# A normalisation kernel at the pace of its DMA engines: early loads cut into halves of 64 partitions, shared by both queues, with 72 transfers in place of 65

## The chip, the cores and the metric

The kernel runs on one core of a Trainium2 chip. The metric is the device time of one execution in microseconds (us). Each run also has a profile of one execution, whose span is some 1.7 to 2.2 us shorter than the device time, since it leaves out what lies around the program.

## The reference

For each of 4 x 8 x 16 = 512 channels of 256 x 256 float32 values, the mean and variance over the channel are taken, and the channel is normalised and scaled:

```python
def reference(x, gamma):                       # x (4, 8, 16, 256, 256), gamma (8, 16)
    mu = x.mean(axis=(3, 4), keepdims=True)
    var = ((x - mu) ** 2).mean(axis=(3, 4), keepdims=True)
    x_norm = (x - mu) / np.sqrt(var + 1e-5)
    return (x_norm * gamma[None, :, :, None, None]).astype(np.float32)
```

134.2 MB are read and 134.2 MB written; each value is needed once.

## The kernel before

A channel is laid over S = 8 partitions, so 16 channels fill a tile of 128 partitions by 8192 float32 values, 4 MiB. There are 32 such units u. Six tiles ("slots", AHEAD = 6) hold units in flight. A unit is loaded into its slot; VectorE sums it, ScalarE sums its squares, TensorE adds the eight partitions of a channel; VectorE scales the tile in place; ScalarE's queue stores it; when the store has landed, SyncE's queue loads unit u + 6 into the slot.

```python
    slots = [data.tile([P, F], F32, name=f"xt{i}") for i in range(AHEAD)]

    def load(u, queue):
        queue.dma_start(out=slots[u % AHEAD][:], in_=xv[u])

    g_row = singles.tile([1, G * C], F32, name="g_row")
    for u in range(AHEAD):
        if u == 1:
            nc.scalar.dma_start(out=g_row[:], in_=gv[None, :])
        load(u, nc.scalar if u in (1, 3) else nc.sync)
    # ... constants and gamma's columns are cut here
    for u in range(U):
        t = slots[u % AHEAD]
        nc.vector.reduce_sum(out=st[:, u, 0:1], in_=t[:], axis=AX.X)
        # ... squares, the small matmul, the root are cut here
        nc.vector.tensor_scalar(
            out=t[:], in0=t[:], scalar1=ps[:, 0:1], scalar2=scale[:, u : u + 1],
            op0=ALU.add, op1=ALU.mult,
        )
        nc.scalar.dma_start(out=ov[u], in_=t[:])
        if u + AHEAD < U:
            load(u + AHEAD, nc.sync)
```

The transfers of the two hardware queues take eight semaphores in turn (the trace has eight that DMAs raise, 128 or 130 times each, 16 times by a large transfer). A transfer that takes a semaphore again waits until its earlier user has landed. The end of the program waits for the eight one after the other (six wait instructions of SyncE between 582.9 and 624.2 us name all eight).

## Time and profile before

| what | value |
|---|---|
| device time | 626.75 us, median of 3 (626.74 to 627.11) |
| span of the profile | 625.2 us |
| large packets (32 KB, one row of one partition) | 8192, so 512 for each of 16 DMA engines |
| median packet | 1213 ns |
| first packet starts | 1.81 us |

The page's DMA row gives the busy share of the 16 engines in tenths for each of 40 equal slices, and the row under it the GB/s that they moved. The first says that the engines have packets in hand, the second how fast those go.

### The profile page before, as it was taken

The page shows a single profiled execution, that of the slowest core. Times are in us where ns is not written, and L with a number is a line of the kernel's source. Part 1 is how long each engine was busy: PE and PEld are TensorE (multiplying, and loading weights), DVE is VectorE, ACT ScalarE, POOL GpSimd, SP SyncE. Part 2 cuts the span into 40 slices and gives each one's busy share as a digit, 9 for nine tenths or more (in the row PEclk, how much of TensorE's full clock was granted, in tenths as well). Part 3 has the DMA queues.
Part 4 walks back from the last instruction along what each step waited for, and adds up shares of the span by engine and source line. Part 5 has one row for each costly group of instructions (what it writes and reads, how often), then busy time and mean ns, then how long its engine had stood idle before and what let it go on. Part 6 is the DMA issues. An engine that isn't in the chain of part 4 may idle for free.

```text
span 625.2 us, 626 instructions
## 1 busy us (share of the span) xinstructions
PE 21.4 (3%) x80; PEld 19.5 (3%) x80; DVE 443.2 (71%) x162; ACT 238.8 (38%) x98; POOL 1.3 (0%) x9
## 2 busy tenths in 40 slices
PE   2000000000000000000000000000000000000000
PEld 2000000000000000000000000000000000000000
DVE  0699999998867668676687766776667867668620
ACT  0444444444444224443244432344423443224400
POOL 0000000000000000000000000000000000000000
DMA  8999999999999999999999999999999999999998
GB/s 369 436 417 424 434 436 436 436 436 437 434 436 434 426 426 430 434 436 436 436 434 434 436 434 434 430 426 430 434 436 436 436 432 434 436 436 434 426 426 365
DMA packets 9220, 268.46 MB, mean 429 GB/s; under 512 B 1025, under 2 KB 1026, under 8 KB 1026
## 3 DMA queue, kind: packets, MB, share of 16 engines
q10 hardware_dynamic: 4898, 142.61, 52.8%
q1 hardware_dynamic: 4320, 125.83, 46.8%
q14 instruction: 2, 0.02, 0.0%
HBM read 134.22 MB, written 134.22 MB: 429 GB/s over the span
## 4 chain that ended last, share of the span: by engine, by line
another core or an unknown queue 64%; DMA 16%; DVE 13%; SPq 1%; PE 1%; issue 0%; ACT 0%
DMA xt<-in_x_dram 9%; DVE st L103 8%; DMA out_dram<-xt 7%; DVE xt L126 4%; SPq L48 1%; PE ps L112 1%; ACT std L117 0%; DVE nvar L113 0%; DVE rstd L121 0%; DVE scale L123 0%
## 5 line engine op out<-in xcount | busy, mean ns | idle before, releaser
L103 DVE TENSOR_REDUCE st<-xt 128x1 f32<-128x8192 f32 x32 | 277.9, 8684 | 111.2 <-DMA xt<-in_x_dram 111.2
L104 ACT ACTIVATE junk<-xt 128x8192 uint8<-128x8192 f32 x32 | 225.0, 7030 | 272.2 <-DMA xt<-in_x_dram 229.0
L126 DVE TENSOR_SCALAR xt<-xt,ps,scale 128x8192 f32<-128x8192 f32 x32 | 145.6, 4550 | 1.2
L117 ACT ACTIVATE std<-nvar,eps_t 128x1 f32<-128x1 f32 x32 | 9.4, 294 | 79.6 <-DVE nvar L113 79.6
L112 PE MATMUL ps<-st,navg 128*128 128x2 f32 x64 | 17.9, 349 | 568.0 <-DVE st L103 568.0
L112 PEld LDWEIGHTS ps<-st,navg 128*128 128x128 f32 x64 | 16.0, 312 | 569.8 <-issue 569.8
L113 DVE TENSOR_SCALAR nvar<-ps 128x1 f32<-128x1 f32 x32 | 9.2, 287 | 23.8 <-PE ps L112 23.8
L121 DVE RECIPROCAL rstd<-std 128x1 f32<-128x1 f32 x32 | 5.3, 164 | 11.6 <-ACT std L117 11.6
L104 ACT ACTIVATION_READ_ACCUMULATOR junk<-xt 128x1 f32 x32 | 6.0, 186 | 0.0
L123 DVE TENSOR_TENSOR scale<-rstd,g_col 128x1 f32<-128x1 f32 x32 | 5.1, 159 | 1.1
L84 PE MATMUL g_ps<-one,g_rep 1*128 1x1 f32 x16 | 3.5, 346 | 2.9 <-DVE g_rep L79 2.9
L84 PEld LDWEIGHTS g_ps<-one,g_rep 1*128 1x128 f32 x16 | 3.5, 325 | 2.9 <-POOL navg L68 2.9
L90 DVE COPY g_col<-g_ps 128x8 f32<-128x8 f32 x1 | 0.2, 166 | 3.7 <-PE g_ps L84 3.7
L74 ACT ACT_TABLE_LOAD x1 | 1.3, 1283 | 2.2 <-issue 2.2
L79 DVE COPY g_rep<-g_row 1x1024 f32<-1x1024 f32 x1 | 0.7, 681 | 2.1 <-DMA g_row<-in_gamma_dram 2.1
L64 POOL TENSOR_SCALAR_AFFINE_SELECT navg<-navg 128x128 f32<-128x128 f32 x1 | 0.4, 403 | 0.1
L68 POOL TENSOR_SCALAR_AFFINE_SELECT navg<-navg 128x128 f32<-128x128 f32 x1 | 0.4, 398 | 0.1
L63 POOL MEMSET navg<- 128x128 f32 x1 | 0.2, 220 | 0.0
L74 ACT ACTIVATE root_eps<-eps_t 128x1 f32<-128x1 f32 x1 | 0.2, 203 | 0.0
L147 POOL MEMSET const-bfloat16-1.0<- 128x1 bf16 x1 | 0.1, 101 | 0.0
L147 POOL MEMSET const-uint8-127<- 128x1 uint8 x1 | 0.1, 101 | 0.0
L147 POOL MEMSET const-float32-0.0<- 128x1 f32 x1 | 0.1, 98 | 0.3 <-issue 0.3
(3 smaller groups left out, 0.3 us busy)
## 6 DMA issues: line engine op xcount, KB each, us to landing
out_dram<-xt ACTq DMA_DIRECT2D x32, 4096.0 KB, 67.1
xt<-in_x_dram SPq DMA_DIRECT2D x30, 4096.0 KB, 33.8
xt<-in_x_dram ACTq DMA_DIRECT2D x2, 4096.0 KB, 33.3
g_row<-in_gamma_dram ACTq DMA_DIRECT2D x1, 0.5 KB
```

The source lines that it names most:

```text
L48: queue.dma_start(out=slots[u % AHEAD][:], in_=xv[u])
L74: nc.scalar.activation(out=root_eps[:], in_=eps_t[:], func=ACTF.Sqrt)
L79: nc.vector.tensor_copy(out=g_rep[:], in_=g_row[:].rearrange("o (n k) -> o n k", n=NG).unsqueeze(3).to_broadcast([1, NG, K, S]),)
L84: nc.tensor.matmul(out=g_ps[:, n : n + 1], lhsT=g_rep[:, n].rearrange("o k s -> o (k s)"), rhs=one[:], start=True, stop=True,)
L103: nc.vector.reduce_sum(out=st[:, u, 0:1], in_=t[:], axis=AX.X)
L104: square = nc.scalar.activation(out=junk[:], in_=t[:], func=ACTF.Square, accum_out=st[:, u, 1:2],)
L112: nc.tensor.matmul(out=ps[:], lhsT=navg_w, rhs=st[:, u], start=True, stop=True)
L113: nc.vector.tensor_scalar(out=nvar[:, u : u + 1], in0=ps[:, 0:1], scalar1=ps[:, 0:1], scalar2=ps[:, 1:2], op0=ALU.mult, op1=ALU.add,)
L117: nc.scalar.activation(out=std[:, u : u + 1], in_=nvar[:, u : u + 1], func=ACTF.Sqrt, bias=eps_t[:], scale=-1.0,)
L121: nc.vector.reciprocal(out=rstd[:, u : u + 1], in_=std[:, u : u + 1])
L123: nc.vector.tensor_mul(out=scale[:, u : u + 1], in0=rstd[:, u : u + 1], in1=g_col[:, g : g + 1],)
L126: nc.vector.tensor_scalar(out=t[:], in0=t[:], scalar1=ps[:, 0:1], scalar2=scale[:, u : u + 1], op0=ALU.add, op1=ALU.mult,)
```

## The change

Its intent, as I read it, is to bring unit 0 in sooner, by loading it (and unit 2) through both queues at once, and to end on the last of the eight semaphores: with the early loads and unit 6 in halves there are 1 + 12 + 2 + 25 + 32 = 72 = 9 x 8 transfers. The halves are halves of the rows, partitions 0 to 63 and 64 to 127.

```diff
-    def load(u, queue):
-        queue.dma_start(out=slots[u % AHEAD][:], in_=xv[u])
+    def load(u, queue, lo=0, hi=P):
+        queue.dma_start(out=slots[u % AHEAD][lo:hi], in_=xv[u, lo:hi])
...
-    for u in range(AHEAD):
-        if u == 1:
-            nc.scalar.dma_start(out=g_row[:], in_=gv[None, :])
-        load(u, nc.scalar if u in (1, 3) else nc.sync)
+    load(0, nc.sync, 0, P // 2)
+    nc.scalar.dma_start(out=g_row[:], in_=gv[None, :])
+    load(0, nc.scalar, P // 2, P)
+    load(2, nc.sync, 0, P // 2)
+    for h in range(2):
+        load(1, nc.scalar, h * P // 2, (h + 1) * P // 2)
+    load(2, nc.scalar, P // 2, P)
+    for u in range(3, AHEAD):
+        for h in range(2):
+            load(u, nc.sync, h * P // 2, (h + 1) * P // 2)
...
         if u + AHEAD < U:
-            load(u + AHEAD, nc.sync)
+            for h in range(2) if u == 0 else [None]:
+                lo, hi = (0, P) if h is None else (h * P // 2, (h + 1) * P // 2)
+                load(u + AHEAD, nc.sync, lo, hi)
```

## The prediction

> **What bounds the kernel now.** I read the page first (busy shares, the 40 slices, the queues), then the windows view at both ends, then the waits of the DMA queue's engine, and last the single packet and semaphore records of the trace. The page:
>
> ```profile
> PE 21.4 (3%) x80; PEld 19.5 (3%) x80; DVE 443.2 (71%) x162; ACT 238.8 (38%) x98; POOL 1.3 (0%) x9
> ...
> DMA  8999999999999999999999999999999999999998
> GB/s 369 436 417 424 434 436 436 436 436 437 434 436 434 426 426 430 434 436 436 436 434 434 436 434 434 430 426 430 434 436 436 436 432 434 436 436 434 426 426 365
> ...
> q10 hardware_dynamic: 4898, 142.61, 52.8%
> q1 hardware_dynamic: 4320, 125.83, 46.8%
> ```
>
> No compute engine is full: VectorE, the busiest, is idle for 29%. The DMA row has a 9 in every slice but the first and last, and the two queues' packets together (q1 is issued by SyncE, q10 by ScalarE) take 99.6% of the 16 engines' time. The packet records say what that time consists of. There are 8192 large packets, each one 32 KB row of one partition; their median duration is 1213 ns, on both queues, to within a few per cent at the 90th percentile. That is 32768 B / 1.213 us = 27.0 GB/s for an engine, 432 GB/s for sixteen. 8192 / 16 = 512 packets for each engine, and 512 x 1.213 = 621.1 us, of a span of 625.2. So the kernel is a bare stream of rows, and only the ends are anything else:
>
> ```profile
> 0.00:2.00 2.00, 0.00 (x0) 0.00 (x0) 0.00 (x0) 0.00 (x0) 1.27 (x9) 1.00 0.65 164
> ...
> 621.00:622.00 1.00, 0.00 (x0) 0.00 (x0) 0.00 (x0) 0.00 (x0) 0.00 (x0) 1.00 1.21 524
> 622.00:623.00 1.00, 0.00 (x0) 0.00 (x0) 0.00 (x0) 0.00 (x0) 0.00 (x0) 1.00 0.23 98
> 623.00:624.00 1.00, 0.00 (x0) 0.00 (x0) 0.00 (x0) 0.00 (x0) 0.00 (x0) 1.00 0.00 0
> ```
>
> The last two columns are DMA share and GB/s. The first row's packet starts at 1.81 us; the last ends in the 622nd microsecond, after which the end of the program takes 3.0 us. At the end SyncE waits for the last store:
>
> ```profile
> SPq L48 <- DMA out_dram<-xt: 536.6, 26, 61.7
> SPq L158 <- DMA out_dram<-xt: 41.1, 1, 41.1
> ```
>
> The 26 waits of L48 are loads that wait for a buffer's store. They cost nothing, because both rings hold several rows for each engine: a load takes 33.8 us from issue to landing and a store 67.1, against 19.3 us for a unit of load and store (two times eight rows at 1.213 us). The 41.1 us are stores draining alone after the last load (landed 582.8), still at full rate, 128 to 137 packets in each 10 us. The semaphore records show the tail exactly: the wait that holds the last store's semaphore ends at 624.06, three more wait instructions follow at 624.10, 624.16 and 624.22, the drain comes at 624.29.
>
> [...] after two rows of unit 0, rows of queue 10 start at 6.13 and of queue 1 at 7.34, one 1.213 us row apart, so unit 0 lands only at 20.3 us though eight rows alone would need 9.7.[...]
>
> **The change part by part.**
>
> Bytes: unchanged, 512 rows for each engine. A half has 64 rows, four for each engine if all sixteen are still used; 621.1 us of rows remain.
>
> Start: SyncE's first issue still starts at 0.8 us (0.33 to 0.53 us each), and ScalarE still issues gamma first. Nothing comes sooner. Unit 0 needs eight rows of an engine in place of about fifteen, so without any new limit it lands near 1.8 + 0.9 (the first rows took about 2.0 us) + 8 x 1.213 = 12.4 us, not 20.3. Its store can be issued some 15 us later (sum, root and scaling took 20.32 to 35.34), but that store only joins a ring that has loads to work on. Gain on the path: 0, since no engine was waiting for it.
>
> Semaphores: there are eight, and in the trace each transfer waits for the earlier user of its own semaphore (ScalarE's waits of 17 ns; SyncE's waits name two). Thirteen transfers now go out before the first store, in place of seven, so the ninth to thirteenth must wait for the first to fifth to land. At that time SyncE's ring still holds the first halves of units 2 and 3, eight rows for each engine. Cost 0. Store 0 has to wait for the second half of unit 1, about 32 us, against 27.5 when it is ready; the ring of ScalarE then still holds half of unit 2. Cost 0. In the steady state stores wait for the store four before, 67.1 us old against 4 x 19.3 = 77.4: as now.
>
> Tail: 72 = 9 x 8 transfers instead of 65 = 8 x 8 + 1, so the last store's wait is the last one; the three that follow now (624.06 to 624.29, less one step of 0.04) fall away: -0.19 us.
>
> Issue: seven more issues at 0.33 us, on sequencers that have nothing else due: 0.
>
> [...] In the order of the rings, the pairs that run together, four rows each, are 0 low with 0 high, 2 low with 1 low, 3 low with 1 high, 3 high with 2 high; then units 4 and 5 and later 6, half by half, beside stores.[...] In the first and third pair (16 rows) the halves are opposite, but packets alternate on each engine, and the sixteen engines run nearly in step (their second rows start within 0.5 us of one another), so they are likely to be all on the low half and then all on the high half[...]. There is no slack to absorb it, the engines being full to the end.
>
> **The rivals.**
>
> A, [...]the row stays at 1.213 us, and the result is 626.75 - 0.19 = 626.6. For it: the change looks like the work of somebody who saw halves do no harm, since the semaphore part is worth only 0.2 us[...]
>
> B, [...]the engines fall out of step elsewhere: 626.6 + 19.4 = 646.0.[...]
>
> C, [...]the engines stay in step: up to 626.6 + 67.9 = 694.5; with the spread taken off (about 0.2 us for each of the 40 rows, my estimate from the start times) about 686. For it: the records show that the engines keep step.
>
> D, the new semaphore waits run a ring dry: one ring empty costs nothing while the other has rows; both would have to be, and I count at least four rows left in each. I give this under 1 us.
>
> E, earlier unit 0 really shortens the run: no view shows a wait of the DMA engines for it; at most a part of the slow rows at 40 to 50 us (queue 1's mean 1338 ns over 80 rows, 0.6 us for each engine). This gives 626 at best.
>
> **Range and chances.** I give A (with D and E) 0.41, B and C together 0.58. The two groups don't touch, so a single number is a choice: I take B, 646, which lies between the others[...]. The range runs from A's 626.2 to a little short of C, 684. Over 2% slower begins at 639.3, which B and C pass and A doesn't: slower 0.58, within 2% 0.41, faster (under 614.2, below the 621.1 us of rows) 0.01.
>
> **What would show it.** [...]in the changed profile the DMA row stays 9 while GB/s falls in the first five or six slices[...], and row packets take over 2 us there; unit 0 lands nearer 20 than 12.4 us. [...]GB/s 430 and more from the second slice, unit 0 at about 12.4 us, and first store landing at about 61 instead of 64.4. Semaphores: SyncE waits on landed loads from 2 to about 32 us, with no dip in the DMA row. Tail: about 0.04 us from the last store's wait to the drain. After about slice 8 all should be as before, a unit each 19.3 us. I am wrong in the main if rows keep 1213 ns in halves, and wrong in another way if slices go under 9.

What the forecast says of half rows rested on a claim that no trace of the kernel before shows, so the claim and the terms that came from it are cut. The terms were guesses: 19.4 us for the second and fourth pair, up to 19.4 us for the first and third, and up to 29.1 us beside stores, in sum 19.4 to 67.9 us. Rival B's 646.0, the number given, is 626.6 with 19.4 us of them, and rival C's 694.5 is 626.6 with all 67.9. In "What would show it", the first sentence has the signs of slow half rows (A is wrong), the second those of half rows at 1.213 us (A is right).

## The result, and the profile after

The changed kernel takes 686.82 us (median of 4, 683.88 to 688.60), the kernel before 626.87 us (median of 4). The ratio is 1.0951, with a 95% interval of 1.0913 to 1.0990: 9.5% slower. Ratios here are the mean time of one kernel's fast runs over that of the other's of the same rounds, so not quite the ratio of the medians that are quoted. The results are correct.

The page of the kernel after, busy shares, DMA row and GB/s, queues:

```profile
PE 21.4 (3%) x80; PEld 19.5 (3%) x80; DVE 443.7 (65%) x162; ACT 238.8 (35%) x98; POOL 1.3 (0%) x9
...
DMA  9999999999999999999999999999999999999997
GB/s 213 209 191 214 214 318 335 341 358 404 437 438 437 431 427 433 431 437 437 437 431 429 431 433 437 437 435 433 431 431 431 435 438 435 431 433 431 431 437 320
...
q10 hardware_dynamic: 4930, 142.61, 51.7%
q1 hardware_dynamic: 4400, 125.83, 47.7%
```

The compute engines did the same work. The DMA row has a 9 in every slice but the last: no queue ran dry. But GB/s is half of before in the first five slices (0 to 86 us) and three quarters in the next four or five; from slice 11 on it is as before. So the engines are as busy as before and slower.

The windows view at the same places, first before, then after (columns: stretch, its length, busy time of PE, PEld, DVE, ACT, POOL with counts, clock, DMA share, GB/s):

```profile
12.00:30.00 18.00, 0.56 (x2) 0.50 (x2) 8.93 (x2) 7.12 (x2) 0.00 (x0) 1.00 1.01 437
...
50.00:78.00 28.00, 1.12 (x4) 1.01 (x4) 25.64 (x11) 14.83 (x6) 0.00 (x0) 1.00 1.00 431
...
110.00:130.00 20.00, 0.56 (x2) 0.50 (x2) 18.82 (x7) 12.06 (x4) 0.00 (x0) 1.00 0.98 421
200.00:220.00 20.00, 0.56 (x2) 0.50 (x2) 14.50 (x6) 8.07 (x4) 0.00 (x0) 1.00 1.01 436
```

```profile
12.00:30.00 18.00, 0.00 (x0) 0.00 (x0) 1.83 (x1) 1.84 (x1) 0.00 (x0) 1.00 1.05 226
...
50.00:78.00 28.00, 0.56 (x2) 0.50 (x2) 8.90 (x2) 7.12 (x2) 0.00 (x0) 1.00 1.00 207
...
110.00:130.00 20.00, 0.56 (x2) 0.50 (x2) 15.50 (x6) 7.33 (x4) 0.00 (x0) 1.00 1.00 328
200.00:220.00 20.00, 0.56 (x2) 0.50 (x2) 14.50 (x6) 8.08 (x4) 0.00 (x0) 1.00 1.02 441
```

The second to last column is about 1.00 in all eight lines (it can pass 1, since this view counts a packet whole where it starts), and only the last differs. The packet records say the same for single rows. In the kernel after, rows between 9.3 and 16.5 us, where SyncE's queue has a low half and ScalarE's a high half, take 2.36 us (48 rows, 2.35 to 2.42); from 20 to 68 us the median is 2.55 us; after 160 us it is 1.213 again.

Adding it up: the rows' time over 16 engines is 622.5 us before and 679.9 us after, a difference of 57.4 us. Of that, 39.4 us were added before 80 us, by 32 rows of each engine, and 17.9 us between 80 and 160 us, where 24 half rows run beside stores (these two parts are the packets' time above 1.213 us a row, after less before). The spans differ by 59.4 us. The other 2 us are a first packet that starts at 2.14 us, not 1.81, and engines that finish less evenly at the end. So all but some 2 us of the loss lies in row packets that are longer.

The waits of SyncE's queue, after:

```profile
SPq L48 <- DMA out_dram<-xt: 537.2, 26, 54.7
...
SPq L48 <- DMA xt<-in_x_dram: 53.0, 4, 19.9
```

The second line is new: the four waits for a semaphore's earlier user. They fall where the DMA row has its 9, so they look free here; the first experiment, which keeps them, shows it. At the end the last store's wait ends at 683.68 and the drain follows at 683.72, 0.04 us later instead of 0.23 us.

### The profile page after: what moved, and what is told of

It is laid out like the page before. It is cut to its first block, busy times and chain, and to the rows that moved or that the text cites. A ratio compares the mean times of both kernels' runs of the same rounds, so it can differ in the third digit from the quotient of the medians.

```text
span 684.6 us, 646 instructions
## 1 busy us (share of the span) xinstructions
PE 21.4 (3%) x80; PEld 19.5 (3%) x80; DVE 443.7 (65%) x162; ACT 238.8 (35%) x98; POOL 1.3 (0%) x9
## 4 chain that ended last, share of the span: by engine, by line
another core or an unknown queue 75%; DMA 10%; DVE 8%; SPq 1%; issue 1%; PE 0%; ACT 0%; ACTq 0%; DVEq 0%
DMA xt<-in_x_dram 10%; DVE st L109 6%; SPq L48 1%; DVE xt L132 1%; PE ps L118 0%; ACT std L123 0%; DVE nvar L119 0%; DVE rstd L127 0%; DVE scale L129 0%; ACTq L53 0%; DVEq L109 0%
## 5 line engine op out<-in xcount | busy, mean ns | idle before, releaser
L118 PE MATMUL ps<-st,navg 128*128 128x2 f32 x64 | 17.9, 349 | 629.9 <-DVE st L109 611.5
L118 PEld LDWEIGHTS ps<-st,navg 128*128 128x128 f32 x64 | 16.0, 311 | 631.7 <-issue 597.9
## 6 DMA issues: line engine op xcount, KB each, us to landing
xt<-in_x_dram SPq DMA_DIRECT2D x25, 4096.0 KB, 38.8
```

Source lines behind the costliest of these rows:

```text
L118: nc.tensor.matmul(out=ps[:], lhsT=navg_w, rhs=st[:, u], start=True, stop=True)
```

## The experiments

**Theory P**: how long a row takes depends on the partitions that its transfer writes, and transfers to 0 to 63, or to 64 to 127, are slow (rows of 2.36 to 2.55 us in the kernel after). The reason for it is shown by no run; row times of 4.85 us are guesses. P has two forms, which part where the two queues carry opposite halves: by the moment (slow if all engines are on the same half at once, in step) or by the mean (opposite halves even each other out). **Rivals**: T, more transfers and their semaphore waits; H, the addresses read in HBM; N, transfers of few partitions are slow as such. Fourteen kernels ran. Row times below are medians of the packet records.

### The same 72 transfers, cut along the columns (`cols`)

```diff
     def load(u, queue, lo=0, hi=P):
-        queue.dma_start(out=slots[u % AHEAD][lo:hi], in_=xv[u, lo:hi])
+        lo, hi = lo * (F // P), hi * (F // P)
+        queue.dma_start(out=slots[u % AHEAD][:, lo:hi], in_=xv[u, :, lo:hi])
```

> The changed kernel with every half cut along the columns (128 partitions, 4096 columns each) in place of the rows: same 72 transfers, same order, same queues, same semaphores. Theory P[...]: the cost of the change is gone, 626.4 to 626.9 us, packets of 16 KB at about 607 ns, unit 0 landed near 12.4 us, and the tail is about 0.2 us shorter. Rival T (more transfers and the semaphore waits between them cost the time): it stays near 686 us.

Measured: 627.88 us against 627.07, ratio 1.0013 (0.9997 to 1.0030). The page's GB/s:

```profile
GB/s 367 427 396 451 418 436 424 432 436 435 431 435 436 435 433 435 435 435 433 433 435 429 429 427 431 435 435 433 435 435 433 433 435 435 435 433 435 435 427 352
```

The slices that were near 210 are near 430, packets of 16 KB take 611 ns, and SyncE's share of unit 0 lands at 10.6, ScalarE's at 15.5 us. With number, order, queues and semaphores the same, T is out: the cost is in the cut along the partitions. Earlier data of unit 0 brought nothing.

### Only units 0 and 2 in row halves (`shared_only`)

```diff
+    load(0, nc.sync, 0, P // 2)
+    nc.scalar.dma_start(out=g_row[:], in_=gv[None, :])
+    load(0, nc.scalar, P // 2, P)
+    load(2, nc.sync, 0, P // 2)
+    load(1, nc.scalar)
+    load(2, nc.scalar, P // 2, P)
+    for u in range(3, AHEAD):
+        load(u, nc.sync)                     # and unit 6 whole
```

> Only units 0 and 2 in row halves on both queues, all other loads whole (67 transfers). Theory P with engines in step (each half row takes about twice 1.213 us whatever the other queue does): 16 half rows for each engine, 16 x 1.2 = 19 us, 646 us. Theory P with engines out of step[...]: unit 0's halves are opposite and cost 0, unit 2's halves beside a whole unit cost about 4.85 us each, 636 us. Rival T, by its share of two of the seven extra transfers: about 644 us, so this run parts only the two forms of P.

Measured: 647.23 us, ratio 1.0321 (1.0301 to 1.0342). Sixteen half rows cost 20 us: unit 0's opposite halves cost about as much as the others. The form by the mean (636) misses.

### Opposite halves only (`opposed`), and shifts (`opposed_shift`, `opposed_one`)

```diff
+    nc.scalar.dma_start(out=g_row[:], in_=gv[None, :])
+    for u in range(4):
+        load(u, nc.sync, 0, P // 2)
+        load(u, nc.scalar, P // 2, P)
+    for u in range(4, AHEAD):
+        load(u, nc.sync)                     # and unit 6 whole
```

> Units 0 to 3 in row halves, always the low half on SyncE's queue and the high half on ScalarE's, units 4 and 5 whole: the two queues never write the same half[...]. Theory P out of step: 627 us. Theory P in step (the engines take turns between the rings at the same moments, so all are on the low half, then all on the high half): 32 half rows for each engine at 2.36 instead of 1.21 us, +37 us, 663 us. Rival T: four of seven extra transfers, 661 us.

Measured: 665.91 us, ratio 1.0619 (1.0598 to 1.0640), rows of 2.40 us: +39 us for 32 half rows. Two of its windows:

```profile
12.00:30.00 18.00, 0.00 (x0) 0.00 (x0) 1.84 (x1) 1.85 (x1) 0.00 (x0) 1.00 1.05 226
30.00:50.00 20.00, 0.56 (x2) 0.50 (x2) 14.43 (x6) 8.06 (x4) 0.00 (x0) 1.00 0.98 210
```

A high half on the other queue gives a low half next to nothing (2.40 us against the 2.55 of equal halves). The two shifted kernels add one line ahead of unit 0:

```diff
+    nc.sync.dma_start(out=slots[5][64:96:4], in_=xv[5, 64:96:4])   # opposed_shift
+    nc.sync.dma_start(out=slots[5][64:65], in_=xv[5, 64:65])       # opposed_one
```

> As the run with opposite halves, but before unit 0 one extra load of eight rows[...] on SyncE's queue, which gives one row to eight engines only and so puts them one row behind the others. If the lockstep is the cause[...]: row packets fall from 2.36 towards 1.21 us and the run ends at 627 to 640 us. If [...]the shift doesn't last, 660 to 665 us. Rival T has one transfer more: about 670 us.

> As the run with opposite halves, with one extra row (one engine alone, partition 64, rewritten later) ahead on SyncE's queue. The shift of eight engines changed nothing[...]. If being out of step doesn't help, all sixteen keep 2.37 us and only one engine is late. Total either way 660 to 670 us, since the slowest engine ends it.

Measured: 667.98 us, ratio 1.0652 (1.0631 to 1.0673), and 682.05 us (one run). The semaphore records show that the shift of eight engines worked in part: eight increments of ScalarE's first half come at 21.3 to 21.7 us and eight at 22.4 to 23.1. So eight engines lag by about half a row. Still rows take 2.38 us in the median of both kernels, and between 12 and 78 us none takes less than 2.36 (up to 2.56 where a queue has two rows in a row). No engine got faster by being late. (Most of the 14 us that `opposed_one` lies above the other come late: SyncE's rows after 160 us average 1.264 us there; why, I can't say.)

### A middle piece of 64 partitions (`middle`)

```diff
+    for u in range(AHEAD):
+        for lo, hi in ((0, 32), (32, 96), (96, 128)) if u < 2 else ((0, P),):
+            load(u, nc.sync, lo, hi)
```

> Units 0 and 1 in three row pieces on SyncE's queue alone: rows 0 to 31, 32 to 95, 96 to 127; the rest whole. The middle piece has 64 partitions like a half[...]. Theory P[...]: rows of the middle piece 1.213 us, rows of the outer pieces about 2.4 us: eight slow rows for each engine, 8 x 1.2 = 9.7 us, 636.5 us. Rival N (any transfer of fewer than 128 rows is slow, by its count of rows or its descriptors): all rows 2.4 us, +19 us, 646 us.

Measured: 640.29 us, ratio 1.0211 (1.0192 to 1.0230), "unclear", since the interval holds the 2% line. Rows of the middle pieces take 1.218 us, those of the outer pieces 2.56 us where they don't overlap a piece of another kind. N is out: 64 partitions that lie across both halves are as fast as a whole tile (1.213 us). The packets above 1.213 us add 9.5 us over the kernel before, as expected; the other 3.5 us or so are a gap at the end, told below.

### The same HBM rows to other partitions (`swap`, wrong result)

```diff
+    def piece(u, p, r, n):
+        nc.sync.dma_start(out=slots[u][p:p + n], in_=xv[u, r:r + n])
+
+    piece(0, 32, 0, 64)
+    piece(0, 0, 64, 32)
+    piece(0, 96, 96, 32)
+    piece(1, 0, 32, 64)
+    piece(1, 64, 0, 32)
+    piece(1, 96, 96, 32)
+    for u in range(2, AHEAD):
+        load(u, nc.sync)
```

> Wrong result on purpose: in unit 0 the rows of HBM that made the low half (0 to 63) go to partitions 32 to 95, in unit 1 rows 32 to 95 go to partitions 0 to 63; the rest of both in pieces of 32. SyncE's queue alone. Theory P (the side of SBUF decides): the first four rows of each engine in unit 0 take 1.213 us, those of unit 1 2.4 to 2.56 us; 4 + 8 slow rows, +14.6 us, 641 us. Rival H (the side of HBM decides, by the addresses that the sixteen engines read at once): the first four rows of unit 0 are slow and those of unit 1 fast.

Measured: 656.03 us (one run). In unit 0 the first rows (HBM rows of the low half, partitions 32 to 95) take 1.217 us in the median, those that start between 4 and 7 us; in unit 1 (rows 32 to 95 of HBM to partitions 0 to 63) they take 2.35 to 2.57 us, those that start between 16.9 and 25.3 us. H is out: the partitions written decide. The total is 15 us above the expectation for two other reasons: some rows after 80 us are slow (5.3 us for an engine, unexplained), and the gap at the end is larger:

```profile
630.00:640.00 10.00, 0.56 (x2) 0.50 (x2) 8.82 (x5) 4.27 (x3) 0.00 (x0) 1.00 0.39 167
```

Here the DMA share itself falls. With all early loads on one queue, later loads queue up on SyncE's ring (whole loads land 69.8 and 73.4 us after their issue in the median of `middle` and `swap`, against 33.8), and stores come through fast. Counted by rows, 3.4 stores are still queued when the last load's rows end in the kernel before, 1.5 in `middle` and 1.0 in `swap`; the last unit's compute, 15.05 us, is as long as 1.55 stores of eight rows. What the stores don't cover stands open. In the kernel before, the last store is issued at 597.9 us, 16 us before the store ahead of it lands; in `middle` at 625.8, 1.8 us after it landed. One queue alone need not bring the gap: `every_other` and `sixteen`, below, load on SyncE's queue alone too, have 2.0 and 1.9 stores left, and lose under 1 us at the end. What sets the split of the backlog was not tested.

### Few partitions at a time (`eight`, `sixteen`)

```diff
+    for j in range(4):                                          # eight
+        nc.sync.dma_start(out=slots[0][j:32:4], in_=xv[0, j:32:4])
+    for lo, hi in ((32, 40), (40, 48), (48, 64), (64, 128)):
+        load(0, nc.sync, lo, hi)

+    for lo in (0, 64, 16, 80, 32, 96, 48, 112):                 # sixteen
+        load(0, nc.sync, lo, lo + 16)
```

> Unit 0 on SyncE's queue in small pieces: four transfers of eight rows[...] (eight engines, one row each), two of eight neighbouring rows[...], one of sixteen neighbouring rows[...], then the high half. Theory P: [...]1.2, then 4.85, 4.85, and 2.4 us. Rival N (few partitions are slow as such): the first four kinds are as slow as a half, or slower, 2.4 us and more.

> Unit 0 as eight transfers of sixteen neighbouring rows, one row for each engine, on SyncE's queue, in the order 0, 64, 16, 80, 32, 96, 48, 112.[...] If what counts is the moment: rows of 4.85 us, +29 us, 656 to 660 us. If an engine evens out its rows over neighbouring transfers: rows near 1.2 us, 627 to 632 us. If two transfers run into one another: between, 2.4 us, about 637 us.

Measured: 652.33 and 652.68 us (one run each). In `eight` the first rows, of every fourth partition from 0 to 31, take 1.37 us in the median with the start in it (1.21 at least), so low partitions alone are not slow. The later transfers overlap, so their rows test no single transfer: by the landing times, the other eight engines begin rows of partitions 48 to 63 at 6.5 us. Of the two transfers of eight neighbouring rows, rows of the first then take about 5.0 us and of the second 3.8. The high half, expected at 2.4 us, takes 3.8 to 4.7 beside them (2.43 after them), though those write low partitions alone; and rows of the whole unit 1 take 3.3 to 3.6 us between 26 and 36 us, while half of the engines are still on the high half. The page's GB/s, in slices of 16.3 us:

```profile
GB/s 143 143 355 435 435 435 427 443 423 439 428 433 435 431 440 425 445 421 431 437 431 439 427 441 427 441 423 431 437 431 439 425 445 423 437 431 429 439 411 290
```

So it seems that slow rows slow those beside them, to other partitions too; no run tests this apart. In `sixteen` every row takes 4.50 us (4.485 to 4.507 from the second transfer on), where 4.85 was a guess; the windows view has

```profile
12.00:22.00 10.00, 0.00 (x0) 0.00 (x0) 0.00 (x0) 0.00 (x0) 0.00 (x0) 1.00 0.91 105
```

a quarter of the rate at a DMA share of 0.91. Neighbouring transfers don't even each other out: the next one always writes the other half, and the rows still take 4.50 us.

### Every other partition (`every_other`)

```diff
+    for u in range(2):
+        for h in range(2):
+            nc.sync.dma_start(out=slots[u][h::2], in_=xv[u, h::2])
+    for u in range(2, AHEAD):
+        load(u, nc.sync)
```

> Units 0 and 1 in two transfers each, of every other row to every other partition[...], on SyncE's queue alone.[...] Theory P in step[...]: rows of about 2.4 us, 16 x 1.2 = 19 us, and up to 4 us more at the end as in the run with the middle piece, where the single loading queue left the last store late: 646 to 650 us. Theory P by the mean[...]: rows 1.213 us, 627 to 631 us.

Measured: 628.22 us, ratio 1.0021 (0.9992 to 1.0051), rows of 1.213 us:

```profile
12.00:22.00 10.00, 0.00 (x0) 0.00 (x0) 8.52 (x1) 7.12 (x2) 0.00 (x0) 1.00 0.97 419
```

The 2.4 us expected in step rested on a guess at which rows of a transfer an engine takes. The records don't name a packet's engine, so that stays open; what is shown is that these 64 partitions cost nothing.

### Halves in turn on one queue (`in_turn`), and with a lag (`in_turn_lag`)

```diff
+    for j in range(4):                                          # in_turn_lag alone
+        nc.sync.dma_start(out=slots[5][64 + j:96:4], in_=xv[5, 64 + j:96:4])
+    for u in range(2):                                          # both
+        for h in range(2):
+            load(u, nc.sync, h * P // 2, (h + 1) * P // 2)
+    for u in range(2, AHEAD):
+        load(u, nc.sync)
```

> Control: units 0 and 1 in row halves, low, high, low, high, all on SyncE's queue, other loads whole; only gamma on ScalarE's. In step: all sixteen engines write the low half, then all the high half: 16 half rows at about 2.5 us, +20 us and up to 4 us more for a late last store, 646 to 652 us. If an engine evens out its rows over the four of a transfer and more, it would be 627 to 631 us.

> The control with four extra loads of eight rows ahead on the same queue (eight engines, one row each per load[...], rewritten later): these eight engines start the first low half four rows later, when the others go on to the high half. If the phase decides[...], all half rows take 1.213 us; the eight engines still have four rows more, 4.9 us: 632 to 637 us. If phase doesn't decide[...], 2.4 to 2.5 us stay: 651 to 658 us.

Measured: 662.73 and 664.09 us (one run each). Rows take 2.56 us in both, and 2.36 to 2.43 (2.39 to 2.53 with the lag) where a half follows the other half. The totals lie 10.7 and 6.1 us above what was expected. In the control, rows before 80 us add 19.7 us over the kernel before, as expected; slow rows after 80 us add another 6.9 us (unexplained), and the rest, about 9 us, is mostly a wider gap at the end. The two faults make the totals a poor measure here, so the row times decide. The lag was smaller than planned: the small transfers' issues of 0.7 us each and the first rows' start ate it up, and the two groups of engines land 1 to 2 us apart, not four rows. So this is a weak test, but that lag, too, made no row faster.

### Halves beside stores alone (`beside_stores`)

```diff
-            load(u + AHEAD, nc.sync)
+            for lo, hi in ((0, 64), (64, P)) if u < 3 else ((0, P),):
+                nc.sync.dma_start(out=slots[u % AHEAD][lo:hi], in_=xv[u + AHEAD, lo:hi])
```

> The kernel before, whole early loads, with units 6 to 8 alone in row halves: 24 half rows for each engine, all beside stores. In the changed kernel such rows cost 18.0 us for 24 (0.75 us each, load and store packets together). If that is the term's size: 645 us. If it is the full lockstep of the prediction, 29 us: 656 us. If halves beside stores are free: 627 us.

Measured: 650.10 us, ratio 1.0371 (1.0321 to 1.0420). 24 half rows cost 23 us, 0.97 us each, more than the 0.75 of the changed kernel and less than a full 1.2. Between 80 and 160 us SyncE's rows average 1.98 us and the stores beside them 1.36, so a small part of a half row's time is won back beside stores, and a part of the cost shows on the stores' packets.

### The intent without the halves (`gamma_pool`)

```diff
-            nc.scalar.dma_start(out=g_row[:], in_=gv[None, :])
+            nc.gpsimd.dma_start(out=g_row[:], in_=gv[None, :])
```

> The kernel before with one edit: gamma's load goes to GpSimd's queue, so that the two hardware queues carry 64 transfers and the last store uses the last of the eight semaphores. This takes the intent of the change without its halves. Theory: the three waits after the last store's wait fall away, 0.16 to 0.19 us, 626.6 us; rival: the tail doesn't set the time, 626.8 us or, if GpSimd's transfer costs something, more.

Measured: 627.13 us (626.62 to 627.41) against 627.05, ratio 0.9998 (0.9984 to 1.0012). In the trace the tail is shorter as intended, 0.04 us from the last wait to the drain, but 0.19 us is less than the spread of its five runs. No kernel beat the one before; its 512 rows of 1.213 us leave some 4 us of a span of 625.2.

## Why the prediction was right or wrong

The direction was right, and so was the place of the cost: rows take about twice as long when a transfer writes partitions 0 to 63 or 64 to 127 (2.35 to 2.58 us for 1.213). Why they do was not shown. The size was wrong. I put 646.0 and a range up to 684.0; measured 686.82.

- **The bound** held. 512 rows of an engine set the time, and no compute engine or ring took over.
- **Equal halves, 19.4 us** (second and fourth pair) held in kind: rows of 2.55 us, 5% over the 2.43 guessed.
- **Opposite halves, "0 to 19.4 us"**: here is the step that failed. I took 0 for the single number (rival B, "the engines fall out of step elsewhere"). They cost 2.36 us a row in the changed kernel, and 2.40 us a row with nothing else in play (`opposed`). Both kinds of pair together, 32 rows, added 39.4 us, against 19.4 in B and 38.8 at the upper end. By the row times, 16 x (2.36 - 1.213) = 18.4 us of the 40.8 us between 646.0 and 686.8 come from this step, and 17.9 us from the next.
- **Beside stores, "0 to 29.1 us"**: again B took 0. Measured 17.9 us in the changed kernel, and 23 us in a kernel with these alone. This term was mis-sized by both rivals.
- **Rival C's 686** came out near the measured time by luck. With its 0.2 us off, each of its 40 rows costs 1.01 us more: 35.6 us before the stores, where 39.4 were measured, and 24.3 beside them, where 17.9 were measured. Nor is its reason what the runs show. If two engines slowed each other only while both had a row, and overlapped by all but an offset d, a row would take 2 x 1.213 - d. In the changed kernel the last of the sixteen engines starts a row at 10.40 us, 0.40 us after the one before it, so its row should take 2.03 us or less whoever its partner is. It took 2.36, as did the fifteen that start between 9.50 and 10.00. Shifts of about 1 us changed nothing either. So the form of P by the moment doesn't hold as I drew it, and the form by the mean fell with `opposed`. What the runs do show is row times by the partitions that a transfer writes: whole tiles, partitions 32 to 95 and every other partition 1.21 to 1.22 us; 0 to 63 or 64 to 127 2.35 to 2.58 us; sixteen neighbouring ones (`sixteen`) 4.50 us; every fourth from 0 to 31 (the start of `eight`) 1.37 us with the start in it. A transfer to the other half beside it is of almost no help (2.40 us for 2.55). Where unlike transfers overlap, in the rest of `eight`, rows took 3.3 to 5.0 us, and these times don't carry over. How the hardware comes to this is open.
- **Start**: the first packet came 0.33 us later, not at the same time: a row half's issue took 0.57 us on SyncE in place of 0.37, which is 0.20 of it. (SyncE's first issue took 0.53 to 0.57 us for 64 rows in five kernels, and 0.37 to 0.39 for a whole tile, a column half, or 32 or 16 rows.)
- **Semaphores and ring depth (rival D)** held: four waits, 53.0 us, with the DMA row at 9, and `cols`, which has four such waits too (26.5 us), is no slower.
- **Tail, -0.19 us** held in the trace: 0.04 in place of 0.23 us.
- **Earlier unit 0 (rival E)** is worth nothing, as said: `cols` has it and is no faster.
- **The signs** given for slow half rows were there: 9 in the DMA row with GB/s near 210, rows over 2 us, unit 0 complete at 28.1 us, later even than the 20 that I named.
- **Two readings were wrong**, without effect on the sum. Three rows of unit 0, not two, run on each engine before the queues take turns. And the last rows end at 623.57 us, not in the 622nd microsecond, so 1.6 us follow them, not 3.0; the windows view had put each packet where it starts.

The chances followed a doubt that was fed by a guess about who had made the change and why: 0.41 for A, half rows that keep 1.213 us. No trace then showed a half row, so neither side had a measurement behind it. And between B and C the number was put "between the others", at a value that B alone would give.

## What to carry to other kernels

When a kernel runs at the pace of its DMA engines, cut a transfer along the columns and keep all 128 partitions (packets of 16 KB at 611 ns in `cols`), or pick 64 partitions such as 32 to 95 or every other one (1.218 and 1.213 us a row); the halves 0 to 63 and 64 to 127 double each row's time (2.35 to 2.58 us), on two queues (2.40 us in `opposed`) as on one (2.56 in `in_turn`). Read GB/s beside the DMA busy share: a full share at half the rate means slow packets (1.00 at 207 GB/s in the kernel after), a low share means a dry queue (0.39 at 167 GB/s in `swap`), and the two want different cures. Look last at how the backlog is split between loads and stores: stores still queued when the last load lands are what covers the last unit's compute (3.4 stores in the kernel before, 1.0 in `swap`).
